# Moving the key and query norms, the gate's order and pair 6's scores in a two-layer attention encoder

## The chip, the cores and the metric

The kernel runs on one core of one Trainium2 chip. TensorE (PE in the profile) multiplies matrices into PSUM banks; VectorE (DVE), ScalarE (ACT) and GpSimd (POOL) work on tiles; SyncE (SP) issues the DMAs. Each engine runs its own instructions in order and waits on semaphores that the others raise. The metric is the device time in microseconds (us), lower is better.

## The reference, cut to what matters

The input is 512 tokens of width 1024, in float32. Two layers follow each other, each with 16 heads of 64.

```python
def reference(x, ...):
    for i in range(2):
        hn = rms_norm(x, norm_gain[i])
        y = mixer_a(hn, ...) if i == 0 else mixer_b(hn, ...)
        x = x + y
    return x

# mixer_a: three dilation groups of q, k, v and one gate, projected from hn
#   q = rms_norm(q, q_gain); k = rms_norm(k, k_gain)        # per head, over 64
#   logits = q . k / 8 + bias[bucket(distance)], masked to the window
#   softmax over the keys; the three groups merged by their denominators
#   y = (merged output) * silu(gate);  return y @ w_out
# mixer_b: one group of q, k, v and one gate; tokens as an 8 x 64 grid
#   logits = q . k / 8 + bias[row distance, column distance], masked to 16 columns
#   y = softmax(logits) @ v * silu(gate);  return y @ w_out
```

## The kernel before

**Arithmetic.** Every large product is done in three matmuls of a reduced float format: an operand is split into a high part and a low remainder, and `mm3` issues high x high, high x low and low x high. Weights arrive by DMA as `wraw`, ScalarE casts the high part `wh` (L127), and VectorE or GpSimd subtracts the low part `wl` (L131; two splits of five go to GpSimd).

**Main stream.** `main()` walks over eight pairs of heads, numbered 0 to 7, in layer A, then the output product of A, then eight pairs in layer B, then the output product of B. A pair of layer A has four projections over eight blocks of 128 input rows: `rawk` (keys of groups 1 and 2 and the values that go with them, 96 matmuls of 512 columns), `rawq` (queries of all groups and the keys of group 0, 96), the values `v0` (24) and the gate (24). Pair 7 does its queries before its keys, and the gate of pair 6 is done inside pair 7. A pair of layer B has 96 matmuls of 384 columns and 24 for its gate. A projection onto tokens keeps four PSUM banks of the pool `ps_acc`, which has four: the next projection's block i can begin only when block i of this one has been evacuated by ScalarE (L427, which also multiplies by the token's norm), and the bank that the gate used is free only when VectorE has evacuated the gate (L457 in layer A, L886 in layer B).

**Side stream.** `side()` is a generator for the attention of each pair. `run` puts its steps between the matmuls of the main stream, by a clock that adds up an assumed cost of each matmul: a `yield n` waits for n ns of that clock, and `yield "wait", key, n` waits until n ns after the event `key`. TensorE's order is exactly what comes out (`manual_schedule`). On the other engines a scheduler orders the instructions by a simulated timeline, except where `keep_in_program_order` fixes them.

**One pair of layer A, in the side stream.** `k_a` transposes the keys on TensorE (`tp<-rawk`, two banks of four transposes) and VectorE copies them out (L489). `q_a` does the same for the queries and the keys of group 0. `attn_a` does the scores in two halves u = 0 and 1: `scores` fills four PSUM banks `log` (76 small matmuls in two steps), VectorE adds the bias and takes the minimum of each row (L700 and L711, "softmax minima"), ScalarE takes the exponentials (L722) and normalises the rows (L560), and VectorE transposes them in blocks of 32 into `tr` (L633), which goes to DRAM and comes back turned as `pt`. `weigh` (`o<-pt,...`) multiplies with the values one pair later, and `put_y` multiplies by the gate (L583), casts the high part `y_h` on ScalarE (L587) and subtracts the low part `y_l` on GpSimd (L588). The banks `log`, `tp` and `o` share a pool of four, `ps_side`.

**Norms.** `squares` sums the squares of each head (GpSimd L268, VectorE L269), `rsqrt` does three Newton steps on 16 values a partition on GpSimd for the keys, and on 32 values on VectorE for the queries (L108 to L116), and `scale` multiplies the four blocks of raw keys or queries (L283). In layer A `scale` is issued as soon as the projection is done, wherever the scheduler puts it; in layer B (`key == "raw"`) it is held in the list `later` and issued behind the evacuation of the gate.

**The gate.** SiLU is computed with tanh: `gt` is the gate times the token norm `rs_all`, `eg` is tanh(0.5 gt), `silu` does gt (eg + 1) in two halves (L553), and `put_y` multiplies by 0.5 and by the output. In layer B the gate is evacuated in the order of the attention's queries (two instructions, 384 and 128 columns, strided), and `put_y` reorders to the grid when it writes `y_h` and `y_l` (two instructions each).

Of the kernel before, what the change touches and what calls it, by code (L numbers as in the profile page):

```python
# [13 lines left out]
F32 = mybir.dt.float32  # L14
# [28 lines left out]
def tile_hybrid_encoder(  # L43
# [228 lines left out]

    later = []

    def head_norm(raw, ss, ns, key):

        rs = wk.tile([P, 32], F32, tag="rs", name="rs")
        rsqrt(nc.vector if ns == 8 else nc.gpsimd, rs[:, : 4 * ns], ss[:, : 4 * ns], 4 * ns, 1.0 / DH)

        def scale():  # L280
            for i in range(4):
                v = raw[:, i, : ns * 64].rearrange("p (a b) -> p a b", b=64)
                m = nc.vector.tensor_mul(  # L283
                    v, v, rs[:, i * ns : (i + 1) * ns].unsqueeze(2).to_broadcast([P, ns, 64])
                )
                if key == "raw":
                    tc.keep_in_program_order(m)

        if key == "raw":
            later.append(scale)  # L290
        else:
            scale()
# [18 lines left out]
    def tjr(t):  # L311
        return t.rearrange("p (t j r) -> p t j r", t=4, j=4)
# [1 line left out]
    ng = cp.tile([P, 2, KT], F32, name="ng")  # L314
    rs_n = cp.tile([P, 4], F32, name="rs_n")
    rs_trj = cp.tile([P, S], F32, name="rs_trj")
    rs_all = cp.tile([P, S], F32, name="rs_all")

    def spread():

# [35 lines left out]

    def scales_a():
        pa = spread()
        nc.scalar.copy(tjr(rs_all), to_tjr(pa))
        nc.scalar.copy(trj(rs_trj), to_trj(pa))  # L360

    def norm(layer, k, xk):
# [73 lines left out]
        normed(raw, ss, ns, key, hc)  # L436

    def normed(raw, ss, ns, key, hc):
        head_norm(raw, ss, ns, key)
        st[key, hc] = raw  # L440
        stamp[key, hc] = clock[0]

# [8 lines left out]
    def gate_a(hc):  # L451
        acc = []
        yield from project_t(acc)
        yield "ya", hc - 2, "y"
        gt = wk.tile([P, S], F32, tag="gt", name="gt", bufs=3)
        eg = wk.tile([P, S], F32, tag="eg", name="eg")
        nc.vector.tensor_mul(tjr(gt), to_tjr(acc[0]), tjr(rs_all))  # L457
        nc.scalar.activation(eg, gt, AF.Tanh, scale=0.5)
        gated(hc, gt, eg)

    def v0_a(hc):
# [19 lines left out]
            yield from gate_a(hc)  # L481

    def k_a(hc):
        yield "wait", ("rawk", hc), 10000 if hc else 12500
        k12 = wk.tile([P, 2, 512], F32, tag="k12", name="k12", bufs=1)
        raw = st.pop(("rawk", hc))
        for g in range(2):
            tp = transpose4(raw, g * P)
            nc.vector.tensor_scalar(k12[:, g, :], tp, gk[:, g + 1 : g + 2], None, op0=ALU.mult)  # L489
            yield  # L490
        st["k12", hc] = k12, raw
        stamp["k12", hc] = 0

    def q_a(hc):
        yield "wait", ("rawq", hc), 13000
        raw = st.pop(("rawq", hc))
        q0h = wk.tile([P, 512], F32R, tag="q0h", name="q0h", bufs=1)
        q0l = wk.tile([P, 512], F32R, tag="q0l", name="q0l", bufs=1)
        q12 = wk.tile([P, 2, 512], F32, tag="q12", name="q12", bufs=1)
        k0h = wk.tile([P, EXT], F32R, tag="k0h", name="k0h", bufs=1)  # L500
        k0l = wk.tile([P, EXT], F32R, tag="k0l", name="k0l", bufs=1)
        tp = transpose4(raw, 0)
        nc.scalar.copy(tjr(q0h), to_tjr(tp))
        nc.vector.tensor_sub(tjr(q0l), to_tjr(tp), tjr(q0h.bitcast(F32)))
        yield
        tp = transpose4(raw, 3 * P)
        put_k([(trj(k0h[:, 64:EXT]), trj(k0l[:, 64:EXT]), to_trj(tp))], 0)
        yield
        for g in range(2):
            tp = transpose4(raw, (g + 1) * P)  # L510
            nc.vector.tensor_copy(tjr(q12[:, g, :]), to_tjr(tp))
            yield
        st["q", hc] = q0h, q0l, q12, k0h, k0l
        stamp["q", hc] = 0
# [27 lines left out]
                matmul(d(o[hs]), v(hs), r(hd), start=(first and i == 0), stop=(i == len(mms) - 1))  # L542

    def gated(hc, gt, eg):
        st["gate", hc] = gt, silu(gt, eg)
        chores.append(st["gate", hc][1])
        stamp["gate", hc] = clock[0]
# [14 lines left out]
    def put_y(hc, o, permuted, last):  # L562

        gt, rest = st.pop(("gate", hc))
        for _ in rest:
            pass
        if permuted:

            pairs = ((lambda t: t.rearrange("p (t ja x) -> p x ja t", t=4, ja=8),
                      lambda t: t.rearrange("p (x ja t) -> p x ja t", t=4, ja=8)),)  # L570
        else:
            pairs = ((mid_cr, mid_n), (edge_cr, edge_n))
        if last and permuted:
            for c in range(4):
                q = slice(P * c, P * c + P)
                of = lambda t: t.rearrange("p (s x) -> p s x", x=16)[:, :, 4 * c : 4 * c + 4]
                nc.vector.scalar_tensor_tensor(of(gt), of(gt), 0.5, of(o), op0=ALU.mult, op1=ALU.mult)
                src = pairs[0][0](gt)[:, 4 * c : 4 * c + 4]
                h, l = (t[:, hc, q].rearrange("p (x ja t) -> p x ja t", x=4, ja=8) for t in (st["y_h"], y_l))
                nc.scalar.copy(h, src)  # L580
                nc.vector.tensor_sub(l, src, h.bitcast(F32))
            return
        nc.vector.scalar_tensor_tensor(gt, gt, 0.5, o, op0=ALU.mult, op1=ALU.mult)  # L583
        eng = nc.vector if last else nc.gpsimd
        for src, dst in pairs:
            h, l = dst(st["y_h"][:, hc, :]), dst(y_l[:, hc, :])
            nc.scalar.copy(h, src(gt))  # L587
            eng.tensor_sub(l, src(gt), h.bitcast(F32))  # L588
        stamp["ya" if permuted else "yb", hc, "y"] = 0

    def bias_a(hc):
# [61 lines left out]
    def attn_a(hc):  # L653
# [39 lines left out]
        def softmax(hd, t, lg, cs, n):  # L693
            pr = wk.tile([P, 512], F32, tag="p", name="p", bufs=4)
            mn = wk.tile([P, 4], F32, tag="mn", name="mn", bufs=4)
            if t == 0:
                nc.gpsimd.memset(pr[:, 0:64], 0.0)
            if t == 3:
                nc.gpsimd.memset(pr[:, 192:256], BIG)
            nc.vector.tensor_tensor_reduce(  # L700
                out=pr[:, cs : cs + n],
                in0=lg[:, cs : cs + n],
                in1=e0[:, hd, cs : cs + n],
                scale=1.0,
                scalar=3.0e38,
                op0=ALU.add,
                op1=ALU.min,
                accum_out=mn[:, 0:1],
            )
            v = lambda t_: t_[:, 256:512].rearrange("p (g c) -> p g c", g=2)  # L710
            nc.vector.tensor_tensor_reduce(  # L711
                out=v(pr),
                in0=v(lg),
                in1=e12[:, 2 * hd : 2 * hd + 2, 96 - 32 * t : 224 - 32 * t],
                scale=1.0,
                scalar=mn[:, 0:1],
                op0=ALU.add,
                op1=ALU.min,
                accum_out=mn[:, 1:2],
            )  # L720
            row = pr[:, cs:512]
            nc.scalar.activation(row, row, AF.Exp, bias=mn[:, 1:2], scale=-1.0, accum_out=mn[:, 2:3])  # L722
            normalise(row, mn)
            return pr
# [31 lines left out]

        if hc < NHC - 1:
            for u in range(2):
                yield 2500 if u == 0 else 16000
                turned = turner(512)  # L760
                turners.append(turned)
                for hd, t, pr in scores(u):
                    turned.put(pr, 512, 256 * hd + 128 * (t % 2))
                later_on(9000, partial(turned.send, pq[:, 2048 * u : 2048 * u + 2048], 11000, 1500))
            pending.append(lambda: put_y(hc, weigh(), True, False))
        else:
            for u in range(2):
# [2 lines left out]
                yield 3200  # L770
                if pending:
                    yield "wait", ("gate", hc - 1), 16800
                    pending.pop()()
                    yield
                for args in held:
                    turn_p(*args)
# [101 lines left out]
    def main_b(hc):  # L878
# [3 lines left out]
        yield ("yb", hc - 3, "y") if hc else ("rs", "all")  # L882
        gt = wk.tile([P, S], F32, tag="gt", name="gt", bufs=3)
        eg = wk.tile([P, S], F32, tag="eg", name="eg")
        for src, dst in ((mid_rc, mid_o), (edge_rc, edge_o)):
            tc.keep_in_program_order(nc.vector.tensor_mul(dst(gt), src(acc[0]), src(rs_all)))  # L886
        while later:
            later.pop()()
        nc.scalar.activation(eg, gt, AF.Tanh, scale=0.5)
        gated(hc, gt, eg)  # L890

    far = lambda hc: hc < NHC - 2

    def side_b(hc):
        if hc >= 2 and far(hc - 2):
            yield "wait", ("raw", hc), 4500
            pending.pop(0)()
            yield
        if hc >= 1 and far(hc - 1):
# [132 lines left out]
    def side():  # L1032
# [20 lines left out]
        for hc in range(NHC):  # L1053
            if hc < NHC - 1:
                yield from k_a(hc)
                yield from chain(q_a(hc), v_a(hc))
                if pending:
                    yield "wait", ("rawq", hc), 21000
                    pending.pop()()
                    yield  # L1060
                yield from attn_a(hc)
                if hc == 2:
# [11 lines left out]
        row_scale(row_sums(st.pop("ssq")))  # L1074
        stamp["rs", "b"] = 0
        yield 5000
        nc.scalar.copy(rs_all, spread())
        stamp["rs", "all"] = 0
        for hc in range(NHC):
            yield from side_b(hc)  # L1080
# [94 lines left out]
```

## Time and profile before

| | |
|---|---|
| time, median of 3 runs | 878.77 us (878.61 to 880.46) |
| the profiled execution | 878.77 us, of which its span is 877.0 us (1.77 us lie around it) |
| TensorE busy | 856.8 us (98%), 5643 matmuls |
| VectorE busy | 514.8 us (59%), 1324 instructions |
| ScalarE busy | 425.2 us (48%), 888 instructions |
| GpSimd busy | 301.8 us (34%), 500 instructions |
| DMA | 128.65 MB, mean 147 GB/s |

In rows of the timeline the first number is the start in us from the start of the span, the second the duration from the first start to the last end, then engine, line, operation, output<-inputs, and the count. A bracket gives the idle time of the engine before the row and what ended it. A matmul's duration holds its passage through the array, so consecutive matmuls overlap: a 512-column one lasts 0.39 us and the next one starts 0.23 us after it.

### The profile page before, as it was taken

Reading aid. Unit: us, or ns where it says so; the run is one execution under the profiler, and the core shown is the slowest. Engines: PE = TensorE matmul, PEld = TensorE weight load, DVE = VectorE, ACT = ScalarE, POOL = GpSimd, SP = SyncE. Lnnn points to the kernel's source line nnn. Section 1 sums busy time; section 2 is a strip of 40 time slices with the busy share of each in tenths; the row PEclk is TensorE's granted clock in tenths of the full one; section 3 lists DMA queues with packets and bytes.
Section 4 is the critical chain, followed back from the end, with each engine's and each line's share of the span. In section 5 each row is a group of like instructions: output and inputs, shape, how many; then the busy total and the mean of one; then the engine's idle time right before and its main releaser. Section 6 shows DMA issues by size and latency. Waiting matters only on the chain.

```text
span 877.0 us, 15515 instructions
## 1 busy us (share of the span) xinstructions
PE 856.8 (98%) x5643; PEld 709.4 (81%) x5643; DVE 514.8 (59%) x1324; ACT 425.2 (48%) x888; POOL 301.8 (34%) x500
## 2 busy tenths in 40 slices
PE   8999999999999999999999899999999999999998
PEld 6788877787787877877778677888988988889786
DVE  7355663663664565466466575528475767766643
ACT  7434533552552552552552554426366646665541
POOL 2341431441531531531442323211443345533611
PEclk9999999999999999999999999999999999999999
DMA  6352672564465465475376275255235654646223
GB/s 243 110 159 74 171 219 77 147 184 133 129 191 146 145 171 150 125 182 160 94 185 188 59 186 149 78 180 189 84 111 160 167 164 150 178 128 188 97 89 128
DMA packets 59708, 128.65 MB, mean 147 GB/s; under 512 B 6384, under 2 KB 23728, under 8 KB 59632
## 3 DMA queue, kind: packets, MB, share of 16 engines
q1 hardware_dynamic: 59344, 127.66, 49.9%
q8 instruction: 44, 0.72, 0.4%
q14 instruction: 32, 0.26, 0.1%
q10 hardware_dynamic: 288, 0.01, 0.0%
HBM read 102.82 MB, written 24.83 MB: 146 GB/s over the span
## 4 chain that ended last, share of the span: by engine, by line
PE 84%; DVE 7%; issue 3%; ACT 2%; POOL 2%; DMA 1%; ACTq 0%; POOLq 0%; DVEq 0%
PE acc L206 70%; PE o L206 4%; PE log L206 4%; PE tp L210 4%; DVE rawq L283 1%; DVE na L115 1%; DVE gt L886 1%; POOL sq L268 1%; POOL wl L131 1%; DVE wl L131 1%; DMA hg<-in_head_gain 1%; ACT p L963 1%; ACT wh L127 0%; DVE rs L116 0%; ACT p L560 0%
## 5 line engine op out<-in xcount | busy, mean ns | idle before, releaser
L127 ACT CAST wh<-wraw 128x512 fp32r<-128x512 f32 (+1 forms) x276 | 161.8, 587 | 301.1 <-PE acc L206 262.3
L206 PE MATMUL acc<-wh,hn_h 128*128 128x512 f32 (+1 forms) x768 | 297.3, 387 | 6.9 <-DVE gt L457 2.5
L206 PE MATMUL acc<-wl,hn_h 128*128 128x512 f32 (+1 forms) x768 | 285.6, 372 | 0.7 <-DVE wl L131 0.7
L206 PE MATMUL acc<-wh,hn_l 128*128 128x512 f32 (+1 forms) x768 | 286.0, 372 | 0.0
L131 POOL TENSOR_TENSOR wl<-wraw,wh 128x512 fp32r<-128x512 f32 (+1 forms) x110 | 137.3, 1248 | 394.5 <-ACT wh L127 346.0
L131 DVE TENSOR_TENSOR wl<-wraw,wh 128x512 fp32r<-128x512 f32 (+1 forms) x166 | 112.2, 676 | 135.8 <-ACT wh L127 131.5
L206 PEld LDWEIGHTS acc<-wh,hn_h 128*128 128x128 f32 x768 | 144.2, 188 | 38.7 <-issue 8.0
L206 PEld LDWEIGHTS acc<-wh,hn_l 128*128 128x128 f32 x768 | 144.2, 188 | 21.0
L206 PEld LDWEIGHTS acc<-wl,hn_h 128*128 128x128 f32 x768 | 144.5, 188 | 18.5 <-DVE wl L131 1.0
L206 PE MATMUL acc<-hn_h,wh 128*128 128x512 f32 x192 | 76.5, 398 | 0.5 <-ACT rawk L427 0.3
L206 PE MATMUL acc<-hn_h,wl 128*128 128x512 f32 x192 | 74.9, 390 | 0.0
L206 PE MATMUL acc<-hn_l,wh 128*128 128x512 f32 x192 | 74.8, 389 | 0.0
L722 ACT ACTIVATE p<-p,mn 128x512 f32<-128x512 f32 (+1 forms) x64 | 44.8, 701 | 55.5 <-DVE mn L711 55.5
L560 ACT ACTIVATE p<-p,mn 128x512 f32<-128x512 f32 (+3 forms) x128 | 68.9, 586 | 0.0
L269 DVE TENSOR_REDUCE ss<-sq 128x4 f32<-128x256 f32 (+1 forms) x96 | 48.3, 504 | 26.2 <-POOL sq L268 25.7
L633 DVE STREAM_TRANSPOSE tr<-p 128x512 f32<-128x512 f32 (+1 forms) x80 | 53.9, 686 | 10.1 <-ACT p L560 8.7
L268 POOL TENSOR_TENSOR sq<-rawk 128x256 f32<-128x256 f32 x64 | 40.4, 640 | 42.1 <-ACT rawk L427 35.8
L206 PE MATMUL acc<-y_h,wh 128*128 128x512 f32 x128 | 52.1, 407 | 0.0
L206 PE MATMUL acc<-y_l,wh 128*128 128x512 f32 x128 | 50.0, 391 | 0.0
L206 PE MATMUL acc<-y_h,wl 128*128 128x512 f32 x128 | 50.0, 390 | 0.0
L283 DVE TENSOR_TENSOR rawk<-rawk,rs 128x256 f32<-128x256 f32 x64 | 40.7, 695 | 15.3 <-POOL rs L120 15.3
L206 PEld LDWEIGHTS acc<-hn_h,wh 128*128 128x128 f32 x192 | 36.2, 188 | 9.9 <-ACT rawk L427 2.7
(130 smaller groups left out, 1087.1 us busy)
## 6 DMA issues: line engine op xcount, KB each, us to landing
wraw<-in_w SPq DMA_DIRECT2D x95, 512.0 KB
wraw<-in_w SPq DMA_DIRECT2D x38, 384.0 KB
td<-tr SPq DMA_DIRECT2D x56, 256.0 KB
pt<-td SPq DMA_DIRECT2D x56, 256.0 KB
td<-tr SPq DMA_DIRECT2D x24, 224.0 KB
pt<-td SPq DMA_DIRECT2D x24, 224.0 KB
e<-l_d SPq DMA_DIRECT2D x32, 112.0 KB
e<-l_d SPq DMA_DIRECT2D x16, 128.0 KB
```

Of the source, the lines that this page charges most:

```text
L115: eng.scalar_tensor_tensor(a[:, :n], a[:, :n], -0.5, v[:, :n], op0=ALU.mult, op1=ALU.mult)
L127: nc.scalar.copy(h, raw)
L131: eng.tensor_sub(l, raw, h.bitcast(F32))
L206: nc.tensor.matmul(o, l, r, **kw)
L210: nc.tensor.transpose(o, i, ident)
L268: nc.gpsimd.tensor_mul(sq, raw[:, i, : ns * 64], raw[:, i, : ns * 64])
L269: nc.vector.tensor_reduce(ss[:, i * ns : (i + 1) * ns], sq.rearrange("p (a b) -> p a b", b=64), axis=AX.X, op=ALU.add)
L283: m = nc.vector.tensor_mul(v, v, rs[:, i * ns : (i + 1) * ns].unsqueeze(2).to_broadcast([P, ns, 64]))
L560: nc.scalar.activation(pr, pr, AF.Copy, scale=mn[:, 3:4])
L633: nc.vector.transpose(dst, src[:, :n].rearrange("p (i b k) -> p i b k", b=4, k=32))
L722: nc.scalar.activation(row, row, AF.Exp, bias=mn[:, 1:2], scale=-1.0, accum_out=mn[:, 2:3])
L886: tc.keep_in_program_order(nc.vector.tensor_mul(dst(gt), src(acc[0]), src(rs_all)))
```

## The change

Layer A, keys of pairs 1 to 6: `scale` is held back, and issued in `k_a` 9500 ns (of the assumed clock) after the projection instead of at once, fixed in program order and after the last softmax minimum that has been issued by then; their transposes wait 18000 ns instead of 10000. Layer A, queries of pairs 0 to 5: `scale` is held back until the gate of the pair has been evacuated, and their transposes wait 15000 ns instead of 13000. The second half of the scores comes 15000 ns after the first instead of 16000. Pair 6: the first half comes 1200 instead of 2500 ns after the step before it, the second 11000 instead of 16000 ns later, and the weighing of pair 5 moves from before the first half to between the halves.

Both layers: the token norms are halved once (`rs_half`), so that tanh and `put_y` need no factor. Layer B: the gate is evacuated in grid order in one instruction, `put_y` reads the output in the other order (two multiplies) and writes `y_h` and `y_l` in one instruction each; the weighing of a pair comes 1500 instead of 4500 ns after the projection two pairs later.

```diff
-    def head_norm(raw, ss, ns, key):
+    def head_norm(raw, ss, ns, held):
...
-                if key == "raw":
+                if held:
                     tc.keep_in_program_order(m)
-        if key == "raw":
+        if held:
             later.append(scale)
         else:
             scale()
...
-        nc.scalar.copy(tjr(rs_all), to_tjr(pa))
+        nc.scalar.mul(tjr(rs_half), to_tjr(pa), 0.5)
...
     def normed(raw, ss, ns, key, hc):
-        head_norm(raw, ss, ns, key)
+        head_norm(raw, ss, ns, key == "raw" or (hc < NHC - 2 if key == "rawq" else 0 < hc < NHC - 1))
...
     def gate_a(hc):
-        nc.vector.tensor_mul(tjr(gt), to_tjr(acc[0]), tjr(rs_all))
-        nc.scalar.activation(eg, gt, AF.Tanh, scale=0.5)
+        tc.keep_in_program_order(nc.vector.tensor_mul(tjr(gt), to_tjr(acc[0]), tjr(rs_half)))
+        while later:
+            later.pop()()
+        nc.scalar.activation(eg, gt, AF.Tanh)
...
     def k_a(hc):
-        yield "wait", ("rawk", hc), 10000 if hc else 12500
+        held = 0 < hc < NHC - 1
+        if held:
+            yield "wait", ("rawk", hc), 9500
+            with tc.issue_after(st["mins"].ins):
+                later.pop()()
+        yield "wait", ("rawk", hc), 18000 if held else 10000 if hc else 12500
...
     def q_a(hc):
-        yield "wait", ("rawq", hc), 13000
+        yield "wait", ("rawq", hc), 15000 if hc < NHC - 2 else 13000
...
     def put_y(hc, o, permuted, last):
...
-        nc.vector.scalar_tensor_tensor(gt, gt, 0.5, o, op0=ALU.mult, op1=ALU.mult)
-        eng = nc.vector if last else nc.gpsimd
-        for src, dst in pairs:
-            h, l = dst(st["y_h"][:, hc, :]), dst(y_l[:, hc, :])
-            nc.scalar.copy(h, src(gt))
-            eng.tensor_sub(l, src(gt), h.bitcast(F32))
+        h, l, src = st["y_h"][:, hc, :], y_l[:, hc, :], gt
+        if permuted:
+            nc.vector.tensor_mul(gt, gt, o)
...
+        else:
+            for grid, line in ((mid_rc, mid_o), (edge_rc, edge_o)):
+                nc.vector.tensor_mul(grid(gt), grid(gt), line(o))
+        nc.scalar.copy(h, src)
+        (nc.vector if last else nc.gpsimd).tensor_sub(l, src, h.bitcast(F32))
...
     def attn_a(hc):
-                yield 2500 if u == 0 else 16000
+                yield (2500 if hc < NHC - 2 else 1200) if u == 0 else 15000 if hc < NHC - 2 else 11000
...
+                if pending and hc == NHC - 2 and u == 0:
+                    yield 2500
+                    pending.pop(0)()
...
     def main_b(hc):
-        for src, dst in ((mid_rc, mid_o), (edge_rc, edge_o)):
-            tc.keep_in_program_order(nc.vector.tensor_mul(dst(gt), src(acc[0]), src(rs_all)))
+        tc.keep_in_program_order(nc.vector.tensor_mul(gt, acc[0], rs_half))
         while later:
             later.pop()()
-        nc.scalar.activation(eg, gt, AF.Tanh, scale=0.5)
+        nc.scalar.activation(eg, gt, AF.Tanh)
...
     def side_b(hc):
-            yield "wait", ("raw", hc), 4500
+            yield "wait", ("raw", hc), 1500
...
     def side():
-                if pending:
-                    yield "wait", ("rawq", hc), 21000
-                    pending.pop()()
+                if pending and hc != NHC - 2:
+                    yield "wait", ("rawq", hc), 22000
+                    pending.pop(0)()
```

More of the change, by code (lines that the diff above doesn't have):

```diff
@@ L316, in tile_hybrid_encoder @@
     rs_trj = cp.tile([P, S], F32, name="rs_trj")
-    rs_all = cp.tile([P, S], F32, name="rs_all")
+    rs_half = cp.tile([P, S], F32, name="rs_half")
     def spread():
@@ L566, in put_y @@
             pass
[L567 to L572, printed above, removed]
         if last and permuted:
@@ L576, in put_y @@
                 of = lambda t: t.rearrange("p (s x) -> p s x", x=16)[:, :, 4 * c : 4 * c + 4]
-                nc.vector.scalar_tensor_tensor(of(gt), of(gt), 0.5, of(o), op0=ALU.mult, op1=ALU.mult)
-                src = pairs[0][0](gt)[:, 4 * c : 4 * c + 4]
+                nc.vector.tensor_mul(of(gt), of(gt), of(o))
+                src = gt.rearrange("p (t ja x) -> p x ja t", t=4, ja=8)[:, 4 * c : 4 * c + 4]
                 h, l = (t[:, hc, q].rearrange("p (x ja t) -> p x ja t", x=4, ja=8) for t in (st["y_h"], y_l))
@@ L582, in put_y @@
             return
-        nc.vector.scalar_tensor_tensor(gt, gt, 0.5, o, op0=ALU.mult, op1=ALU.mult)
-        eng = nc.vector if last else nc.gpsimd
-        for src, dst in pairs:
-            h, l = dst(st["y_h"][:, hc, :]), dst(y_l[:, hc, :])
-            nc.scalar.copy(h, src(gt))
-            eng.tensor_sub(l, src(gt), h.bitcast(F32))
+        h, l, src = st["y_h"][:, hc, :], y_l[:, hc, :], gt
+        if permuted:
+            nc.vector.tensor_mul(gt, gt, o)
+            src = gt.rearrange("p (t ja x) -> p x ja t", t=4, ja=8)
+            h, l = (t.rearrange("p (x ja t) -> p x ja t", t=4, ja=8) for t in (h, l))
+        else:
[3 more added lines that the diff above has]
+        (nc.vector if last else nc.gpsimd).tensor_sub(l, src, h.bitcast(F32))
         stamp["ya" if permuted else "yb", hc, "y"] = 0
@@ L710, in softmax @@
             v = lambda t_: t_[:, 256:512].rearrange("p (g c) -> p g c", g=2)
-            nc.vector.tensor_tensor_reduce(
+            i = nc.vector.tensor_tensor_reduce(
                 out=v(pr),
@@ L720, in softmax @@
             )
+            st["mins"] = i
             row = pr[:, cs:512]
@@ L1056, in side @@
                 yield from chain(q_a(hc), v_a(hc))
-                if pending:
-                    yield "wait", ("rawq", hc), 21000
-                    pending.pop()()
+                if pending and hc != NHC - 2:
+                    yield "wait", ("rawq", hc), 22000
+                    pending.pop(0)()
                     yield
@@ L1076, in side @@
         yield 5000
-        nc.scalar.copy(rs_all, spread())
+        nc.scalar.mul(rs_half, spread(), 0.5)
         stamp["rs", "all"] = 0
```

## The prediction

> **What bounds the kernel.** I read the page first, then the waits of TensorE, then the timeline around each wait. Page, head and slices:
>
> ```profile
> span 877.0 us, 15515 instructions
> PE 856.8 (98%) x5643; PEld 709.4 (81%) x5643; DVE 514.8 (59%) x1324; ACT 425.2 (48%) x888; POOL 301.8 (34%) x500
> ...
> PEclk9999999999999999999999999999999999999999
> ```
>
> TensorE is busy for 98% of the span at full clock, and the change neither adds nor removes a matmul. So only TensorE's waits can change. Its longest waits (in total, times, longest):
>
> ```profile
> PE tp L210 <- DVE mn L711: 6.5, 6, 1.5
> PE acc L206 <- DVE gt L457: 2.5, 5, 0.5
> PE acc L206 <- ACT rawq L427: 2.4, 3, 1.6
> ...
> PE acc L206 <- DVE gt L886: 1.2, 5, 0.2
> ```
>
> An idle time counts from the end of the last matmul, which drains after the next one should have started, so each wait costs a little more. Timeline, first gate wait:
>
> ```profile
> 130.28 0.39 PE L206 MATMUL acc<-wh,hn_l 128*128 128x512 f32 x1
> 131.18 0.50 PE L206 MATMUL acc<-wh,hn_h 128*128 128x512 f32 x1 [0.50 <-DVE gt L457]
> ...
> 128.02 2.50 DVE L283 TENSOR_TENSOR rawq<-rawq,rs 128x512 f32<-128x512 f32 x4
> 130.44 0.68 DVE L457 TENSOR_TENSOR gt<-acc,rs_all 128x512 f32<-128x512 f32 x1
> ```
>
> Start to start 0.90, where 0.23 is usual (0.231 below): 0.67 lost, 0.17 over the idle time. VectorE scales the queries for 2.50 in front of the gate, whose bank TensorE wants.
>
> **What goes.** (1) Gate of layer A: the gate now stands ahead of the four scalings, ends some 0.9 after its last matmul (0.2 to start, 0.68), and TensorE wants the bank nine matmuls, 2.1, after it. All five waits go: 2.5 + 5 x 0.17 = **-3.3**. The scaled queries are wanted 24 matmuls, 5.5, after the gate's end and are done at 0.8 + 2.5 = 3.3: free.
>
> (2) Gate of layer B:
>
> ```profile
> 705.46 1.75 PE L206 MATMUL o<-pt,rawk 128*64 128x128 f32 x24
> ...
> 707.26 0.69 DVE L583 SCALAR_TENSOR_TENSOR gt<-gt,o 128x512 f32<-128x512 f32 x1 [0.71 <-PE o L206]
> 707.87 1.21 DVE L886 TENSOR_TENSOR gt<-acc,rs_all 128x384 f32<-128x384 f32 x2
> 709.00 3.62 DVE L283 TENSOR_TENSOR rawk<-rawk,rs 128x256 f32<-128x256 f32 x4
> ...
> 708.94 1.90 POOL L588 TENSOR_TENSOR y_l<-gt,y_h 128x384 fp32r<-128x384 f32 x2 [0.52 <-ACT y_h L587]
> ```
>
> The gate stands behind a multiply that waits for `o`. With `o` 15 matmuls (3.5) ahead of the gate's end and one contiguous evacuation (0.68, as L457), the five waits go: 1.2 + 5 x 0.17 = **-2.0**. Two strided multiplies in place of L583 should cost what the two strided L886 did, 1.21. In the new order up to two block transposes and a `wl` stand with them ahead of the gate:
>
> ```profile
> L633 DVE STREAM_TRANSPOSE tr<-p 128x384 f32<-128x384 f32 x12 | 6.9, 578 | 0.9 <-ACT p L560 0.4
> L131 DVE TENSOR_TENSOR wl<-wraw,wh 128x384 fp32r<-128x384 f32 x51 | 28.3, 556 | 33.0 <-ACT wh L127 32.4 <-issue 0.6
> ```
>
> 1.2 + 2 x 0.58 + 0.56 = 2.9 of the 3.5: hidden. Without that cover at most the 2.0 would come back. One cast and one subtraction in place of two lie beside other work.
>
> (3) Pair 7's queries: ScalarE evacuates them among pair 6's exponentials. The scores now come 12 matmuls sooner, and the weighing of pair 5 lies behind them; the chain of waits and the groups have its length and that of the cast that it feeds:
>
> ```profile
> 142.01 3.62 PE o L206 x48
> ...
> L587 ACT CAST y_h<-gt 128x512 fp32r<-128x512 f32 x7 | 7.7, 1096 | 0.0
> ```
>
> From the scores' start the last bank is wanted at 2.0 + 21 x 0.231 + 3.6 + 9 x 0.231 = 12.5. Blocks 0 to 2 are evacuated by 11; block 3 stands behind the cast of `y_h` (multiplied by about 11, cast to 12.1) and is ready at 12.9, 0.4 late. 2.4 + 3 x 0.17 = 2.9, less 0.4: **-2.5**. Their transposes now come nine matmuls (2.1) behind the scores instead of at once, so one of the six `tp` waits goes, about 0.9 + 0.3 drain: **-1.2**. Sum so far -9.0.
>
> **Keys of pairs 2 to 6.** A second half of the scores before (start L = 306.38), TensorE, ScalarE, VectorE, GpSimd:
>
> ```profile
> 306.38 0.39 PE L206 MATMUL log<-k0h,q0h 64*128 64x256 f32 x2
> 309.33 0.63 PE L210 MATMUL tp<-ident,rawk 128*128 128x128 f32 x4 [0.91 <-DVE mn L711]
> ...
> 309.22 0.72 ACT L722 ACTIVATE p<-p,mn 128x512 f32<-128x512 f32 x1 [4.15 <-DVE mn L711]
> 313.35 1.32 ACT L560 ACTIVATE p<-p,mn 128x512 f32<-128x512 f32 x2
> 314.57 0.60 ACT L127 CAST wh<-wraw 128x512 fp32r<-128x512 f32 x1
> 315.08 0.72 ACT L560 ACTIVATE p<-p,mn 128x512 f32<-128x512 f32 x1
> ...
> 305.33 2.50 DVE L283 TENSOR_TENSOR rawk<-rawk,rs 128x256 f32<-128x256 f32 x4 [2.20 <-POOL rs L120]
> 315.41 0.65 DVE L131 TENSOR_TENSOR wl<-wraw,wh 128x512 fp32r<-128x512 f32 x1
> 315.98 0.70 DVE L633 STREAM_TRANSPOSE tr<-p 128x512 f32<-128x512 f32 x1
> ...
> 305.26 1.29 POOL L131 TENSOR_TENSOR wl<-wraw,wh 128x512 fp32r<-128x512 f32 x1
> ```
>
> The transposes stood right behind the scores and waited for a minimum to free a bank. The six waits cost 6.5 + 6 x 0.27 (a small matmul's drain) = 8.1; without pair 7's 1.2, 6.9 go. But the scaling, done before L until now, is fixed in program order: in the instruction order of the changed kernel all four stand not just behind the minima but behind the four block transposes of `p` and a `wl` as well, and the transposes on TensorE, 30 projection matmuls behind the scores (39 in pair 1), wait for them one by one. When are they due? The scores last 2.0 and a matmul takes 0.231 (next fence), so TensorE arrives at L + 2.0 + 30 x 0.231 = L + 8.9. When are they done? First exponential at L + 2.84; four of them at 0.72, three normalisations at 0.61, a cast 0.51 and the last normalisation 0.72 end at L + 8.8. VectorE: third transpose to 8.3, `wl` to 8.9, fourth transpose to 9.55 (0.64 each before the next), scaling from there 0.60 each, the fourth done at 9.55 + 1.8 + 0.7 = 12.05. TensorE starts its fourth transpose at 12.1 instead of 8.9 + 3 x 0.11 = 9.25: 2.9 late. Five pairs 14.5, and pair 1, 2.1 later at the transposes, 0.7: 15.2 - 6.9 = **+8.3**. Per pair the bounds are 1.7 (cast and `wl` out of the chain) and 4.0: L283 took 3.62 beside `y_l` of GpSimd, 1.1 over its usual time. I take 2.9, since at 305.33 it began beside a GpSimd `wl` and took 2.50. [...]
>
> **Keys' evacuation, pairs 2 to 6.** A first half of the scores before (L = 286.39):
>
> ```profile
> 289.11 0.67 ACT L722 ACTIVATE p<-p,mn 128x448 f32<-128x448 f32 x1 [2.63 <-DVE mn L711]
> ...
> 286.39 0.36 PE L206 MATMUL log<-k0h,q0h 64*128 64x192 f32 x2
> 288.38 0.50 PE L206 MATMUL acc<-wh,hn_h 128*128 128x512 f32 x1
> 296.00 0.45 PE L206 MATMUL acc<-wh,hn_h 128*128 128x512 f32 x1
> ...
> 293.48 1.33 ACT L560 ACTIVATE p<-p,mn 128x512 f32<-128x512 f32 x2
> 295.23 2.40 ACT L427 ACTIVATE rawk<-acc,rs_n 128x512 f32<-128x512 f32 x4
> ```
>
> 33 matmuls stand between the scores and the end of the key projection (7.62, 0.231 each), and the queries' first matmul, at L + 9.6, finds its bank just evacuated: no wait, and no slack. Because the queries' transposes moved by nine matmuls, so did the scores: now there are 24, and the bank is wanted at L + 2.0 + 5.5 = 7.5. In ScalarE's new order the evacuations follow the third normalisation, with the fourth between the first two. The third starts at L + 7.09 as before, the first evacuation at 7.70, done at 8.37; TensorE follows 0.06 behind such an end:
>
> ```profile
> 497.51 0.67 ACT L427 ACTIVATE rawq<-acc,rs_n 128x512 f32<-128x512 f32 x1
> ...
> 498.24 0.50 PE L206 MATMUL acc<-wh,hn_h 128*128 128x512 f32 x1 [1.58 <-ACT rawq L427]
> ```
>
> So block 0 starts at 8.43, 0.9 late; block 1 is wanted at 9.12, evacuated from 7.70 + 0.58 + 0.61 = 8.89, starts at 9.62, 0.5 more; blocks 2 and 3 are in time. 1.4 a pair, in pairs 2 to 6 (pair 1 has 33): **+7.0**. Bounds a pair: 0.5 (exponentials half a normalisation sooner) and 2.0 (one more cast in front).
>
> **Sum.** -9.0 + 8.3 + 7.0 = +6.3. Against the execution's own time, span 877.0 and 1.77 around it, which is the median 878.77 too: **885.1**.
>
> **Rivals.** (a) The other side: the scaling is served in time, as the new position is meant to allow. It decides at the last normalisation: if it ends by L + 5.6, 3.2 sooner, no key transpose waits, and the 6.9 are won: 878.8 - 9.0 - 6.9 + 7.0 = 869.9. Against it: four exponentials and four normalisations alone take 4 x 0.72 + 3 x 0.61 + 0.72 = 5.4 from L + 2.84 on. 5%. (b) Only the evacuation turns out in time, 878.8 - 9.0 + 8.3 = 878.1. For it, the rows' zero slack could hide an earlier readiness; against it, the seven instructions from 289.11 to 293.48 fill 4.37, 0.62 each. 9%. (c) GpSimd's `wl` blocks the scaling in all six pairs, 1.1 each: 891.7. 8%. (d) The waits, 2.9 in one place, lower the granted clock. Cold matmuls of the same size took:
>
> ```profile
> L345 PE MATMUL busy<-ones x9: 628/628/794, 1.5 to 5.0; 128*128 128x512 f32 x9
> ```
>
> If a stretch as long as these nine (5.0 - 1.5 = 3.5) at 0.63 in place of the 0.39 above followed each of five waits, 3.5 x (1 - 0.39 / 0.63) = 1.3 each: 891.6. Against it, the 1.5 idle waits left PEclk at 9 everywhere, and a transpose comes every 0.6 in the new wait. [...] 3%. The forecast itself keeps 75%.
>
> **How the numbers follow.** The bounds of the two costs are 5 x 1.2 for the keys and 5 x 0.75 for the evacuation to either side, not both at once; about 4 each way: 881.0 to 889.5, some of (c) out of it above, (a) and (b) below. A measurement can tell about 0.2%, 1.8 us. Faster by that: (a) and a little of (b), 0.06; within it: most of (b), and low forecasts, 0.10; slower: 0.84.
>
> **What would show it.** In the waits of TensorE: no `gt` line, `tp` waiting for `rawk` L284 about 12 to 15 in all, `acc` waiting for `rawk` L428 about 5 to 6. In the timeline: four scalings behind the last block transpose, with four TensorE transposes 0.6 apart after them; the first and second query blocks of pairs 2 to 6 behind an evacuation. Wrong would be: keys scaled before TensorE arrives, or a third wait of some us that none of these rows holds.

## The result and the profile after

The changed kernel takes 893.97 us in the median (891.8 to 894.39, 5 runs), beside 880.2 of the kernel before in the same session: a ratio of 1.0158, 95% interval 1.0142 to 1.0175. It is slower, as forecast, but by 13.8 instead of 6.3, and above the range (881.0 to 889.5). The profiled execution took 893.38, its span 891.4. Head and clock slices of its page:

```profile
span 891.4 us, 15495 instructions
PE 869.0 (97%) x5643; PEld 716.4 (80%) x5643; DVE 520.8 (58%) x1323; ACT 421.0 (47%) x880; POOL 296.6 (33%) x493
...
PEclk9999999999999999999999999999999999999999
```

TensorE has the same 5643 matmuls, but is busy for 12.2 longer. Longer busy time for equal work points to slower matmuls, and the clock slices hide them: each averages over 22 us. TensorE's waits (in total, times, longest):

```profile
PE tp L210 <- DVE rawk L284: 9.8, 5, 2.0
PE acc L206 <- ACT rawk L428: 4.9, 11, 0.7
PE busy L346 <- DVE warm L335: 1.5, 1, 1.5
PE acc L206 <- DVE gt L458: 0.6, 1, 0.6
```

The five waits for the gate in each layer, pair 7's query waits and the waits for a minimum are gone; the two forecast waits have come. The timeline at the first key wait, TensorE, VectorE and GpSimd:

```profile
181.59 0.39 PE L206 MATMUL acc<-wh,hn_l 128*128 128x512 f32 x1
183.94 1.39 PE L210 MATMUL tp<-ident,rawk 128*128 128x128 f32 x4 [1.97 <-DVE rawk L284]
184.99 0.77 PE L206 MATMUL acc<-wh,hn_h 128*128 128x512 f32 x1
185.56 0.63 PE L206 MATMUL acc<-wl,hn_h 128*128 128x512 f32 x1
185.99 0.63 PE L206 MATMUL acc<-wh,hn_l 128*128 128x512 f32 x1
...
181.84 0.70 DVE L641 STREAM_TRANSPOSE tr<-p 128x512 f32<-128x512 f32 x1
182.47 2.33 DVE L284 TENSOR_TENSOR rawk<-rawk,rs 128x256 f32<-128x256 f32 x4
...
182.25 1.26 POOL L131 TENSOR_TENSOR wl<-wraw,wh 128x512 fp32r<-128x512 f32 x1 [1.38 <-ACT wh L127]
```

The wait is as foreseen: four scalings behind the last block transpose. What follows is not: matmuls of 0.63 that start 0.43 apart, where 0.39 and 0.23 are usual. The busy times by stretch, with the granted clock (the number after POOL's busy time and count):

```profile
181.27:184.68 3.41, 1.43 (x7) 0.66 (x5) 3.41 (x7) 0.91 (x2) 1.26 (x1) 1.00 0.47 117
184.68:188.09 3.41, 3.41 (x10) 2.55 (x10) 0.87 (x2) 0.16 (x1) 0.00 (x0) 0.50 0.68 142
188.09:191.51 3.42, 3.42 (x18) 2.86 (x17) 1.78 (x3) 2.73 (x5) 1.51 (x2) 1.00 0.91 333
```

For 3.41 after the wait TensorE runs at half clock. The clock record of the trace has this five times, once behind each key wait of pairs 2 to 6, at 184.68, 256.36, 328.04, 399.72 and 471.40, and nowhere else between the start and the end of the span. The evacuation wait, TensorE and ScalarE:

```profile
160.17 0.39 PE L206 MATMUL acc<-wh,hn_l 128*128 128x512 f32 x1
161.26 0.50 PE L206 MATMUL acc<-wh,hn_h 128*128 128x512 f32 x1 [0.70 <-ACT rawk L428]
...
162.44 0.50 PE L206 MATMUL acc<-wh,hn_h 128*128 128x512 f32 x1 [0.22 <-ACT rawk L428]
...
159.91 0.72 ACT L569 ACTIVATE p<-p,mn 128x512 f32<-128x512 f32 x1
160.54 0.67 ACT L428 ACTIVATE rawk<-acc,rs_n 128x512 f32<-128x512 f32 x1
161.11 0.71 ACT L569 ACTIVATE p<-p,mn 128x512 f32<-128x512 f32 x1
161.72 1.82 ACT L428 ACTIVATE rawk<-acc,rs_n 128x512 f32<-128x512 f32 x3
```

ScalarE's order is the forecast one, third normalisation, evacuation, fourth, evacuation.

The table counts, in the two profiled executions, the time from each matmul's start to the next one's over what is usual for that pair of instructions, in us against the kernel before.

| | forecast | measured |
|---|---|---|
| gates, layer A and B | -3.3, -2.0 | -3.3, -2.0 |
| pair 7: queries, their transposes, its keys | -2.5, -1.2, 0 | -2.9, -1.2, -0.5 |
| transposes behind the scores, five waits | -6.9 | -6.9 |
| key wait (2.13 + 0.14 + 0.23 + 0.23 a pair) | +15.2 | +13.6 |
| evacuation (0.86 + 0.39 a pair) | +7.0 | +6.3 |
| half clock behind the key wait (1.65 a pair) | 0 | +8.3 |
| a wait for the last gates (L458) | 0 | +0.7 |
| first microseconds (matmuls 0.43 apart until 10.5, 0.23 in the kernel before) | 0 | +1.5 |
| sum | +6.3 | +13.6 (span +14.4; 0.8 is in no row) |

### The profile page after: what moved, and what is told of

Read it like the earlier page. It is cut to its first block, busy times and chain, and to the rows that moved or that the text cites. A ratio compares the mean times of both kernels' runs of the same rounds, so it can differ in the third digit from the quotient of the medians.

```text
span 891.4 us, 15495 instructions
## 1 busy us (share of the span) xinstructions
PE 869.0 (97%) x5643; PEld 716.4 (80%) x5643; DVE 520.8 (58%) x1323; ACT 421.0 (47%) x880; POOL 296.6 (33%) x493
## 4 chain that ended last, share of the span: by engine, by line
PE 86%; ACT 6%; DVE 5%; issue 1%; DMA 1%; SPq 0%; ACTq 0%; DVEq 0%
PE acc L206 71%; PE o L206 5%; PE tp L210 5%; PE log L206 5%; ACT p L731 2%; ACT p L569 2%; DVE p L708 1%; DVE p L719 1%; ACT rawk L428 1%; DVE rawk L284 1%; DVE tr L641 1%; ACT wh L127 1%; DMA pt<-td 1%; DMA hg<-in_head_gain 1%; ACT p L974 0%
## 5 line engine op out<-in xcount | busy, mean ns | idle before, releaser
L206 PE MATMUL acc<-wh,hn_h 128*128 128x512 f32 (+1 forms) x768 | 300.4, 391 | 5.5 <-ACT rawk L428 4.6
L206 PE MATMUL acc<-wl,hn_h 128*128 128x512 f32 (+1 forms) x768 | 288.8, 376 | 0.4 <-DVE wl L131 0.4
L206 PE MATMUL acc<-wh,hn_l 128*128 128x512 f32 (+1 forms) x768 | 289.1, 376 | 0.0
L131 DVE TENSOR_TENSOR wl<-wraw,wh 128x512 fp32r<-128x512 f32 (+1 forms) x166 | 118.5, 714 | 129.5 <-ACT wh L127 125.3
L206 PEld LDWEIGHTS acc<-wh,hn_h 128*128 128x128 f32 x768 | 146.4, 191 | 36.8 <-ACT rawk L428 9.1
L206 PEld LDWEIGHTS acc<-wh,hn_l 128*128 128x128 f32 x768 | 146.0, 190 | 21.7
L206 PEld LDWEIGHTS acc<-wl,hn_h 128*128 128x128 f32 x768 | 146.3, 191 | 18.9 <-DVE wl L131 0.9
L641 DVE STREAM_TRANSPOSE tr<-p 128x512 f32<-128x512 f32 (+1 forms) x80 | 54.6, 689 | 12.2 <-ACT p L569 11.3
L268 POOL TENSOR_TENSOR sq<-rawq 128x512 f32<-128x512 f32 x32 | 33.2, 1057 | 45.4 <-ACT rawq L428 37.2
```

The source lines that it names most:

```text
L131: eng.tensor_sub(l, raw, h.bitcast(F32))
L206: nc.tensor.matmul(o, l, r, **kw)
L268: nc.gpsimd.tensor_mul(sq, raw[:, i, : ns * 64], raw[:, i, : ns * 64])
L641: nc.vector.transpose(dst, src[:, :n].rearrange("p (i b k) -> p i b k", b=4, k=32))
```

## The experiments

Theory A: the key wait costs twice, 2.7 a pair as a wait and 1.65 as half clock behind it, so whatever takes the wait away is worth 22. Theory B: the half clock has another cause and stays. Each ratio below is to the kernel before in the same session; 0.001 is 0.9 us.

### Keys not held

```diff
-        head_norm(raw, ss, ns, key == "raw" or (hc < NHC - 2 if key == "rawq" else 0 < hc < NHC - 1))
+        head_norm(raw, ss, ns, key == "raw" or (key == "rawq" and hc < NHC - 2))
...
-        if held:
-            yield "wait", ("rawk", hc), 9500
-            with tc.issue_after(st["mins"].ins):
-                later.pop()()
```

> The changed kernel with the keys of pairs 1 to 6 no longer held: they are scaled as soon as the scheduler places them, as before the change; their transposes stay at 18000. Theory A (the key wait costs twice, 2.7 a pair of wait and 1.6 of matmuls at half clock behind it): both go, 893.9 - 5 x 2.7 - 5 x 1.65 = 872, no granted clock below 1 after the start. Theory B (the half clock has another cause, such as the length of the run or its start, and stays): only the wait goes, 893.9 - 13.6 = 880, with the clock still dropping five times. The evacuation wait (6.3) stays by both.

872.23, ratio 0.9916 (0.9899 to 0.9933). Its longest wait, and its span and mean granted clock:

```profile
PE acc L206 <- ACT rawk L428: 4.9, 11, 0.7
...
core 0: 870.6 us, clock 1.000
```

No key wait, no half clock behind the start, and 21 us less than the changed kernel: theory A to the microsecond.

### Keys directly behind the last minimum

```diff
-                if held:
+                if held and fixed:          # fixed = (key != "rawk")
                     tc.keep_in_program_order(m)
```

> The changed kernel with the keys' scaling not fixed in program order, only behind the last minimum: in VectorE's order it now stands in front of the block transposes instead of behind them. If the transposes and the wl ahead of it were what made it late, the key wait and the half clock both go: about 872, as with unheld keys; the third and fourth reciprocal now stand behind 2.4 of scaling, which could give back up to 1 a pair: 872 to 877. If the scaling were late for its own data (rs), nothing changes: 894.

871.52, ratio 0.9908 (0.9893 to 0.9923). VectorE and TensorE:

```profile
175.64 0.47 DVE L719 CUSTOM_DVE_ANT_1 p<-log,e,mn 128x256 f32<-128x256 f32 x1
176.03 0.09 DVE L719 DVE_READ_ACCUMULATOR2_ANT mn<- 128x1 f32 x1
176.03 1.43 DVE L284 TENSOR_TENSOR rawk<-rawk,rs 128x256 f32<-128x256 f32 x4
...
180.40 0.60 PE L210 MATMUL tp<-ident,rawk 128*128 128x128 f32 x4
```

One call, the fixing in program order, decided 22 us: without it the scaling stands behind the last minimum and in front of the transposes, and is done 3 us before TensorE comes. The two reciprocals behind it cost nothing that shows.

### The key wait filled with matmuls

```diff
-    def transpose4(raw, c):
+    def transpose4(raw, c, fill=0, more=0):
...
         for i in range(4):
+            for _ in range(more if i else fill):
+                nc.tensor.matmul(tp, ones[:, :P], ones, start=True, stop=True)
             transpose(tp[:, i * P : (i + 1) * P], raw[:, i, c : c + P])
...
# in k_a: fill = 8 for the first bank (g == 0) of pairs 2 to 6, and 0 for all others
```

> The changed kernel with eight matmuls of 512 columns of ones put into the key wait of pairs 2 to 6 (ahead of the first key transpose, into the same bank, which the transposes overwrite): 40 matmuls more, nothing moved. Theory A: TensorE is busy for 1.85 of the 2.1 that it idled, the clock stays at 1, and the 1.65 of slow matmuls a pair go although work was added: 893.9 - 8 = 886. Theory B: the clock drop has nothing to do with the idle time: 893.9 to 895.

885.44, ratio 1.0071 (1.0046 to 1.0095): 40 matmuls of 512 columns more, and some 8 us less than the changed kernel. Span and mean granted clock:

```profile
core 0: 886.5 us, clock 1.000
```

This kernel keeps the wait's length (2.29 from the start of the last projection matmul to that of the first key transpose, 2.35 in the changed kernel) and loses only the half clock. With the run before it, it splits the 22 into 14 of waiting and 8 of clock, and shows the cause: with 1.98 of matmuls in the wait, the clock stayed at 1.000.

### Which wait lowers the clock

Two more fillings, two matmuls of ones ahead of each of the transposes 2 to 4 and none ahead of the first, and two ahead of the first alone. In the former the fillers overwrite the keys transposed just before them in the bank, so the scores of these pairs come from other numbers; the work and its order stay.

> The changed kernel with two matmuls of ones of 512 columns ahead of the second, third and fourth key transpose of pairs 2 to 6, none ahead of the first: the long idle time of 2.0 stays in one piece, the three short ones (0.1 to 0.2) are filled; the key wait itself keeps its length. If the total idle time near the wait decides the clock (2.6 a pair before, 2.0 now, where the kernel before had 1.8 at most and no drop), the drop may go: 886. If one idle time of 2.0 is enough: the drop stays, 894.

892.12, ratio 1.0143 (1.0113 to 1.0172). All five pairs of the profiled execution had the same wait of 1.97, but only two had the half clock, so neither idea's result came (that the time is near 894 is chance: the fillers lengthened a pair by 1.1, to the 71.13 below without a drop, from 71.7 less 1.65). The stretches of 3.41 around four of the waits (two that drop, two that don't), and the transposes at the end of the first three:

```profile
178.90:182.31 3.41, 1.45 (x8) 0.94 (x7) 3.41 (x6) 1.39 (x3) 1.36 (x2) 1.00 0.57 130
182.31:185.73 3.42, 3.42 (x12) 2.42 (x11) 0.80 (x3) 0.00 (x0) 0.00 (x0) 0.50 0.60 153
250.58:253.99 3.41, 2.22 (x10) 1.50 (x8) 3.22 (x5) 2.42 (x5) 1.06 (x2) 1.00 1.07 285
253.99:257.41 3.42, 2.64 (x14) 2.14 (x15) 2.23 (x5) 0.00 (x0) 0.35 (x1) 1.00 0.55 128
322.26:325.67 3.41, 1.67 (x8) 1.06 (x6) 3.41 (x5) 1.87 (x4) 1.42 (x2) 1.00 0.66 147
393.94:397.35 3.41, 1.44 (x7) 0.93 (x7) 3.41 (x6) 1.31 (x3) 1.27 (x2) 1.00 0.59 137
397.35:400.77 3.42, 3.42 (x11) 2.46 (x10) 0.87 (x3) 0.00 (x0) 0.00 (x0) 0.50 0.33 101
```
```profile
182.06 0.30 PE L210 MATMUL tp<-ident,rawk 128*128 128x128 f32 x1 [1.97 <-DVE rawk L284]
...
254.77 0.30 PE L210 MATMUL tp<-ident,rawk 128*128 128x128 f32 x1 [1.97 <-DVE rawk L284]
...
325.90 0.30 PE L210 MATMUL tp<-ident,rawk 128*128 128x128 f32 x1 [1.97 <-DVE rawk L284]
```

The clock's changes lie on a grid of 3.413 from the first rise on (in the changed kernel the rise is at 10.60, 51 cells ahead of the drop at 184.68; here the two drops are 63 cells apart), and the stretches above are cells of it. Where the whole wait lay in one cell, TensorE was busy for 1.44 to 1.45 of 3.41 and the next cell was at half clock; where an edge cut the wait (at 253.99 and at 325.67), no cell was that empty and nothing dropped. The run also prices a drop without any other kernel: from the first wait's end to the second's, with a drop between, 72.71; from the second's to the third's, with none, 71.13; 1.58.

> The changed kernel with two matmuls of ones ahead of the first key transpose of pairs 2 to 6: the long idle time falls from 2.0 to about 1.6, under the longest (1.5 to 1.8) of the kernel before, which had no drop; the three short ones stay, 2.2 in all. If one long idle time decides: no drop, 886. If the total decides with a limit between 1.8 and 2.2: the drop stays, 894.

892.79, ratio 1.0151 (1.0129 to 1.0174), not the 886 of the first idea: the wait is cut to 1.4, below the longest of the kernel before, and still four of five pairs drop. The cells of the first three; the first and the third are followed by a drop, the second is not:

```profile
180.96:184.37 3.41, 1.99 (x9) 1.05 (x7) 3.41 (x7) 0.91 (x2) 1.26 (x1) 1.00 0.46 114
252.64:256.05 3.41, 1.98 (x9) 1.06 (x7) 3.41 (x7) 1.00 (x2) 1.26 (x1) 1.00 0.99 201
324.32:327.73 3.41, 2.09 (x9) 1.35 (x10) 2.99 (x5) 0.00 (x0) 0.96 (x1) 1.00 0.30 99
```

So the longest idle time is not what counted. Nor is the idle time in all, the second idea, as far as the profile shows it: a cell that was busy for 2.09 was followed by a drop, while one of 1.98 here and one of 1.67 in the run above were not. What decides it for a cell with transposes stays open.

### The evacuation wait

To the kernel with unheld keys:

```diff
-        yield "wait", ("rawq", hc), 15000 if hc < NHC - 2 else 13000
+        yield "wait", ("rawq", hc), 13000
...
-                    yield "wait", ("rawq", hc), 22000
+                    yield "wait", ("rawq", hc), 21000
```

> As the run with unheld keys, and the queries' transposes and the weighing back at 13000 and 21000, which puts 33 instead of 24 matmuls between the first half of the scores and the end of the key projection. If the evacuation wait of the keys comes from these nine matmuls alone, 1.25 a pair goes: 6.3 below the run with unheld keys, about 866, and no wait for rawk L428 is left. If ScalarE is late for another reason, at least 3 of it stays.

866.67, ratio 0.9845 (0.9828 to 0.9863), 6 less than with unheld keys alone:

```profile
PE tp L210 <- DVE rawq L284: 1.1, 4, 0.3
PE acc L206 <- DVE gt L458: 0.6, 1, 0.6
```

The nine matmuls were the cause. Four transposes of queries now wait a little, 0.49 each from start to start, and the later 15000 had spared them that.

### The gains one by one

The queries, on the kernel before (`held` for `rawq` in `head_norm`, `keep_in_program_order` on layer A's gate and `later` emptied behind it):

> The kernel before with one part of the change: the queries of pairs 0 to 5 are scaled behind the evacuation of the pair's gate, which is fixed in VectorE's order. Their transposes stay at 13000. The prediction's term: the five gate waits of layer A go, -3.3. Rival: the transposes, nine matmuls sooner than in the changed kernel, now meet the scaling (four rawq waits of 0.49 stood in the run with unheld keys and wider spacing), so that 2.0 come back: -1.3.

877.37, ratio 0.9965 (0.9953 to 0.9977): -3.1, with -2.0 to -4.1 as the interval. The forecast -3.3 lies in it and the rival's -1.3 does not, but the agreement is in part luck: two of the four rawq waits are there (0.49 each from start to start), and the single wait for the last gates (0.75) comes with this part, so that the waits by themselves make only -1.6. What the rest is stays open.

Layer B, the changed kernel with layer A's order put back (the halved norms stay):

> The changed kernel with layer A put back to the positions of the kernel before (nothing held there, waits of 10000, 13000, 21000, 2500 and 16000), so that the halved norms and layer B's gate in grid order with its earlier weighing are left. The prediction's term: the five gate waits of layer B go, -2.0 against the kernel before. Rival: the two strided multiplies and the earlier weighing cost TensorE as much at the o bank, 0.

878.31, ratio 0.9974 (0.9964 to 0.9985): -2.3, for a forecast of -2.0.

Pair 6, on the kernel before:

> The kernel before with one part of the change: pair 6's scores at 1200 and 11000, the weighing of pair 5 between them. The prediction's term: pair 7's query waits go but 0.4, -2.5, and one wait of the q7 transposes, -1.2: together -3.7. Rival: the wait of 0.74 for the last gates in the output product of A, which the changed kernel and all its variants show and the kernel before doesn't, comes from this part: -3.0.

875.76, ratio 0.9942 (0.9928 to 0.9955): -5.1, more than the forecast -3.7, which lies outside the interval (-4.0 to -6.3). By the waits of the table above this part is worth -2.9 - 1.2 - 0.5 = -4.6. Its waits have no rawq line at all, and no wait for the last gates, which refutes the rival:

```profile
PE tp L210 <- DVE mn L711: 5.6, 5, 1.5
PE acc L206 <- DVE gt L457: 2.5, 5, 0.5
PE busy L345 <- DVE warm L334: 1.5, 1, 1.5
```

### Three versions

Keys behind the minima, queries and weighing at 13000 and 21000:

> A version meant to beat both kernels: keys scaled directly behind the last minimum, queries' transposes and weighing at 13000 and 21000. It has neither the key wait, nor the half clock, nor the evacuation wait. By theory A 871.5 - 6.3 + up to 2.0 of rawq waits: 865 to 867. If the scaling in front of two reciprocals costs something that the evacuation wait has covered, 868 to 870.

867.05, ratio 0.9846 (0.9831 to 0.9861), the upper end of the 865 to 867 expected: in one pair the gate of layer A is late again, by 0.9. The same, with the queries at 13500:

> The version with keys behind the last minimum, the queries' transposes at 13500 and the weighing at 21000: three matmuls later than in the version with 13000, 30 instead of 33 between the scores and the end of the key projection. The rawq waits (three of 0.49) should go and up to 0.2 of evacuation wait a pair should come: 865 to 867, not to be told from 867.05 unless the 1.0 of the late gate goes too.

869.33, ratio 0.9876 (0.9856 to 0.9897), which misses its 865 to 867. The two intervals still touch, but the waits say why it should be slower: at 30 matmuls instead of 33 the evacuation wait is back with 0.64 a pair, not 0.2, and the weighing waits once, 0.8, for its DMA. Last, the changed kernel with the key transposes at 21000 instead of 18000:

> The changed kernel with one number altered: the key transposes of pairs 1 to 6 wait 21000 instead of 18000. TensorE comes to them 48 instead of 30 matmuls behind the scores, 4.2 later; the scaling stays fixed behind the block transposes. By theory A the wait (2.7 a pair) is covered and the half clock goes with it: 872; the scores also move by three matmuls, 0.7, which takes up to 0.7 of the evacuation wait's 0.86 for block 0 and the 0.39 for block 1: down to 867. If the held scaling costs by itself (VectorE's order), more than 872.

874.96, ratio 0.9933 (0.9909 to 0.9958). The key wait and the half clock are gone with the scaling where it was, so the wait is a matter of when TensorE comes. But it missed its 867 to 872, for new waits came elsewhere:

```profile
PE acc L206 <- ACT rawk L428: 6.1, 6, 1.2
PE o L206 <- DMA wraw<-in_w: 1.8, 1, 1.8
PE busy L346 <- DVE warm L335: 1.5, 1, 1.5
PE o L206 <- DMA pt<-td: 1.3, 1, 1.3
```

The weighing comes three matmuls sooner and meets transfers that have not landed, and the evacuation wait, in another order on ScalarE, is 1.32 a pair instead of less. The kernel with unheld keys and the one with the keys behind the minima, both with 33 matmuls (866.67 and 867.05), beat the kernel before by 1.5% and the changed one by 3%.

## Why the prediction was wrong

**What goes: right.** Every wait forecast to go went. Pair 7 was undersized: no 0.4 was left of the query waits, and two small waits of its keys (0.23 each) went as well.

**Key wait: right, a tenth too large.** The scaling began 9.57 behind the scores' start (forecast 9.55) and took 2.33. The wait was 2.72 a pair for 2.9, and pair 1 had none.

**Evacuation: right**, 1.25 a pair for 1.4.

**The half clock: the step that failed.** Rival (d) had this very mechanism, at 3% and with 1.3 a drop; it is the case, with 1.65. Two arguments put it out of the sum. "The 1.5 idle waits left PEclk at 9 everywhere" was read from slices of 22 us, on which the changed kernel, with five drops, shows 9 everywhere too. For the kernel before the conclusion happened to be true in the profiled execution, whose clock record has no drop; two other executions of it, 882.4 and 882.48, list a mean granted clock of 0.995, where the five drops of the changed kernel make 0.990, so it may drop at times too (no trace of these was kept). And a wait of 1.5 that had passed was no bound for another setting: drops followed waits of 1.97 here, and of 1.4 in the run with two fillers ahead of the first transpose. "A transpose comes every 0.6" took small transposes for work that would keep the clock up; the cell that held three of them was followed by the drop all the same. The mechanism was named, and its chance was set too low. Its price was too low because it was worked out from durations; from the starts, 0.23 and 0.43 apart, the same working gives 3.41 x (1 - 0.23 / 0.43) = 1.6. Adding 8.3 to the forecast gives 893.4. That this meets the 893.38 of the profiled execution is partly luck: the other terms of the forecast were 3.2 too high together, and the last gates (0.7), the start (1.5) and the 0.8 in no row made up for it.

**The range: too narrow by its own bounds.** The key wait alone was given 1.2 a pair, 6 in all, to either side; the range took about 4 for both costs together.

**Rival (c): misread.** The prediction took 2.50 for four scalings beside a `wl` of GpSimd as their usual time and so as evidence against (c). Four in the changed kernel, and four behind the minima (minimum, median, maximum in ns):

```profile
L284 DVE TENSOR_TENSOR rawk<-rawk,rs x4: 411/412/1329, 182.5 to 184.4; 128x256 f32<-128x256 f32 x4
```
```profile
L284 DVE TENSOR_TENSOR rawk<-rawk,rs x4: 419/421/423, 176.0 to 177.0; 128x256 f32<-128x256 f32 x4
```

The latter four took 1.43 together, and so did four in the kernel before at 101.01, where GpSimd ran nothing but a memset that ended at 101.15. In the changed kernel the first took 1329 ns, and ended 0.3 after GpSimd's `wl` (182.25 to 183.51). The 2.50 of before held one such long scaling (1491 ns, beside a `wl`), the 3.62 three (1422, 781 and 1229, beside two `y_l` and a `wl`). So every scaling above 700 ns in these rows had a GpSimd operation beside it; why it is long there isn't shown. The sum wasn't hurt, for the row used already held one of them; but 0.9 of every key wait is the long scaling (1329 to 1332 in all five, for 412), and "0.60 each" was wrong: TensorE's transposes came 0.34 apart.

## What to carry to other kernels

When a change adds a wait to the engine that bounds a kernel, look for what follows it as well as for its length: here 2.7 of waiting brought 1.65 of half clock. Read a clock from stretches as short as the wait, never from the page's slices, and an operation's usual time from single instructions without a neighbour, not from a group's total. And a call that only fixes an order can be worth more than everything the change meant to gain: see what stands ahead of the fixed instruction.

## What the runs showed of the hardware

The clock's changes came on a grid of 3.413 whose phase differed from run to run (drops at 184.68 in the changed kernel, at 182.31 and 184.37 in the two with two fillers: 0.36, 1.40 and 0.05 past a multiple of it), so the same wait was hit or spared. In the changed kernel the drops were 71.68 apart, 21 cells exactly, while a pair took 71.7 to 71.8 with its drop: the phase held, and all five were hit. In the kernel with two fillers ahead of each of the later transposes a pair took 72.7 or 71.1, the phase ran away, and three of five were spared. The four executions of that kernel list mean granted clocks of 0.997, 0.996, 0.995 and 0.991 for 890.45, 892.15, 892.09 and 895.44 us, as if the number of drops differed from one to the next.

The start varies likewise. Two kernels that are alike there, the filled one and the one with keys behind the minima (PE's count of matmuls stands behind its busy time; the clock column has no record this early in the former):

```profile
9.00:13.00 4.00, 4.00 (x11) 3.04 (x11) 3.68 (x6) 3.87 (x8) 1.39 (x1) 1.00 1.04 417
```
```profile
9.00:13.00 4.00, 4.00 (x19) 3.34 (x18) 3.67 (x5) 4.00 (x8) 1.40 (x1) 1.00 1.04 411
```

Eleven matmuls against nineteen in the same 4 us: the clock rose at 13.5 in the one and at 5.5 in the other. That is 1.8 us that no edit explains, in kernels whose own times spread by 2 to 4 (878.6 to 882.5 for the kernel before). How much of that spread is the start and how much is drops isn't shown.
